# Products of the identity with itself, put on TensorE's queue at four changes of stage

## The chip, the core and the metric

The kernel runs on one core of a Trainium2 chip, as one launch. The metric is the device time of that launch in microseconds (us), the median of several runs. In the profile the engines are called PE (TensorE, its matrix products), PEld (TensorE's weight loads), DVE (VectorE), ACT (ScalarE), POOL (GpSimd) and SP (SyncE, which here only issues DMAs).

## What is computed

Two blocks of a network on 256 tokens of width 1024, in float32. The first block is windowed attention and pooling. The second has two layers, and its context of another 256 tokens runs beside the latent tokens. Layer 0 mixes by retention and gated linear attention, layer 1 by attention inside a window. Both layers end in the same two steps, and here the change sits:

```python
def second_block(x, c, ctx, c_ctx, ...):
    for i in range(2):
        h  = x  * (1 + sc1)  + sh1
        hc = xc * (1 + csc1) + csh1
        y  = mixer(h, hc)                 # layer 0: retention and GLA, layer 1: window attention
        x  = layer_norm(alpha * x + g1 * y, ...)
        x  = layer_norm(alpha * x + g2 * (square(relu((x * (1 + sc2) + sh2) @ w1)) @ w2), ...)
        # layer 0 does the same two lines for xc
    return x
```

## The kernel before, in words

**Products.** Every large weight is loaded as float32 (`raw`), cast on ACT into a high part `whi` and subtracted on DVE into a low part `wlo` (lines 135 and 136). Activations are split in the same way. A product of two such pairs is three matrix products, `mm3` (lines 159 to 161). `gemm_b` makes tokens x columns for one tile T of 128 tokens, `col_part` makes columns x tokens. Products that accumulate have a bank of PSUM each: `bank(tag)` gives one of 3 banks `mm`, 2 banks `S`, 2 banks `T` and 1 bank `O`.

**Order.** The program is written engine-free, and a scheduler sets each engine's order from the order of writing and from its own estimate of when operands are ready. TensorE then takes its products in that order. `tc.issue_after(x)` is the one instrument that pins: what is issued under it stands behind `x` on its engine. `queued[...]` keeps the last instruction of a kind for that use.

**The step between two stages.** A residual tile is normalised on DVE (`ln_stats` line 360, `ln_norm` line 374, with the power -0.5 on POOL in between). `modulate` (line 333 on) turns it for the next products: eight transposes on TensorE in two lots of four, each lot into a bank `T` (line 195); ACT scales and shifts them out of the bank into `hf` (line 342); DVE makes the high part (line 345) and the low part (line 346) of `h`. Token tiles 0 and 1 are the context, 2 and 3 the latent tokens.

**The four places.** I call them A to D.

- A, start of the MLP of layer 0. `proj_out` ends with the transposes of tiles 0, 1 and 2 (`mod0`); then the first products of `up(0)` run into four banks `os_` (two `mm`, two `S`), context half first; tile 3 is transposed in between.
- B, start of layer 1. The MLP of layer 0 ends with tiles 2 and 3 normalised and modulated, then tiles 0 and 1 are normalised (`normed(0)`, `normed(1)`) and `after(0)` modulates tile 0 (`y` in the profile's names). Layer 1 begins with K for the latent tokens into the banks `kb_` (`mm<-hCh,whi`), V for tiles 2 and 3 (`mm<-whi,hCh`), then K and V for the context and Q for the first heads (`rot_q(0)`, `rot_q(1)`). Tile 1 is modulated inside that stage. `put_q` moves Q by DMA (`Q<-qr`).
- C, the first `window` of attention: scores of Q with K into two banks `S` (line 1289), softmax on DVE and ACT (lines 1296 to 1308), transposes, products with V (line 1316).
- D, start of the MLP of layer 1. `proj_out` gives tiles 2 and 3 (`r`), `mod2` modulates tile 2 inside it and tile 3 behind it. `up(0)` makes tokens x 512 columns by `gemm_b` for tile 2, then for tile 3 (`mm<-whi,hDh`), takes relu and square on ACT (`f`, lines 1067 and 1068), transposes them (`T<-ident,f`) and splits them into `fx`. `down(0)` multiplies `fx` by the second weight.

Of the kernel before, what the change touches and what calls it, by code (L numbers as in the profile page):

```python
# [19 lines left out]
P = 128  # L20
D = 1024
S = 256
# [73 lines left out]
def body(tc, a, cst, out):  # L96
    nc = tc.nc
    with ExitStack() as ctx:
# [7 lines left out]
        def bank(tag):  # L106
            return psum.tile([P, 512], F32, tag=tag, name=tag, bufs={"mm": 3, "S": 2, "T": 2, "O": 1}[tag])
# [13 lines left out]
        queued = {}  # L121
# [35 lines left out]
        def mm3(o, lhs, rhs, first, last):  # L157
            (lh, ll), (rh, rl) = lhs, rhs
            nc.tensor.matmul(o, lh, rh, start=first, stop=False)  # L159
            nc.tensor.matmul(o, lh, rl, start=False, stop=False)  # L160
            queued["mm"] = nc.tensor.matmul(o, ll, rh, start=False, stop=last).ins  # L161

        def col_part(o, ws, j, xs_):

# [11 lines left out]
        def gemm_b(ws, xh, xl, t):  # L176

            n = ws[0][0].shape[-1]
            o = bank("mm")[:, :n]
            for k, w in enumerate(ws):  # L180
                mm3(o, (xh[:, k, t * P:(t + 1) * P], xl[:, k, t * P:(t + 1) * P]), w, k == 0, k == len(ws) - 1)
            return o
# [8 lines left out]
        ident = const.tile([P, P], F32, tag="ident", name="ident")  # L191
        neghalf = const.tile([P, 8], F32, tag="neghalf", name="neghalf")

        def transpose(o, i, n=P):
            return nc.tensor.transpose(o, i, ident[:n, :n])  # L195

        def rsqrt(v, n):

# [131 lines left out]
            nc.vector.tensor_add(B, B, sh[:, :, vec])  # L330
            return A, B

        def modulate(z, cols, dst, t0):

            A, B = cols
            for c in range(0, KC, 4):
                pt = bank("T")
                hf = tmp([P, 4, P], "hf")
                for i in range(4):
                    transpose(pt[:, i * P:(i + 1) * P], z[:, (c + i) * P:(c + i + 1) * P])  # L340
                for i in range(4):
                    queued["hf"] = nc.scalar.activation(hf[:, i, :], pt[:, i * P:(i + 1) * P], AF.Identity, scale=A[:, c + i:c + i + 1],  # L342
                                                        bias=B[:, c + i:c + i + 1]).ins
                hi, lo = (t[:, c:c + 4, t0:t0 + P] for t in dst)
                nc.vector.tensor_copy(hi, hf)
                queued["mod"] = nc.vector.tensor_sub(lo, hf, hi.bitcast(F32)).ins  # L346
# [183 lines left out]
        for g in range(3):  # L530
            oh = tmp([33, 384], "oh")
            nc.gpsimd.dma_start(oh, cst["oh"][:, g, :])
            pt = bank("S")
# [18 lines left out]
        for g in range(3):  # L552
# [4 lines left out]
            for i in range(2):  # L557
                o = gemm_a(w_in, 1536 * g + 256 * i, xk) if g else first[i].rearrange("p (j n) -> p j n", j=2)
# [112 lines left out]
        for i in range(2):  # L671
# [3 lines left out]
            for j in range(2):  # L675
                g = 2 * i + j
# [374 lines left out]
        def mlp(layer, Ts, xks, y, pool, mid, late, norm, after):  # L1051


            n = len(Ts) * P
            w1, w2 = a["mlp_w1_2"][layer], a["mlp_w2_2"][layer]
            def up(g):

                if g == 3:
                    rate[0] = 3
                fx = (main, pool)[g % 2].tile([P, 8, n], F32R, tag=("qkb", "fx")[g % 2], name="fx")  # L1060
                fh, fl = fx[:, 0:4], fx[:, 4:8]
                if layer and g < 1:
                    ws = w_b(w1, 512 * g)
                    for i in range(2):
                        o = gemm_b(ws, *h2, i)
                        f = pool.tile([P, 512], F32, tag="f", name="f", bufs=2)
                        nc.scalar.activation(f, o, AF.Relu)
                        nc.scalar.activation(f, f, AF.Square)
                        pt = bank("T")
                        for c in range(4):  # L1070
                            transpose(pt[:, c * P:c * P + P], f[:, c * P:c * P + P])
                        tv = pt.rearrange("p (c n) -> p c n", c=4)
                        split(fh[:, :, i * P:i * P + P], fl[:, :, i * P:i * P + P], tv)
                os_ = [bank("mm" if i < 2 else "S")[:, :n] for i in range(4)] if not layer and g == 0 else None
                if not layer and g == 0:
                    ws = [w_a(w1, 256 * i) for i in range(2)]
                    for part, xk_ in xks[0]:
                        for i in range(2):
                            for j in range(2):
                                col_part(os_[2 * i + j][:, part], ws[i], j, xk_)  # L1080
                            mid()
                for i in range(0 if layer and g < 1 else 2):
                    if g:
                        ws = w_a(w1, 512 * g + 256 * i)
                    for j in range(2):
                        if g:
                            o = bank("mm")[:, :n]
                            col_part(o, ws, j, xks[1])
                        else:
                            o = os_[2 * i + j]  # L1090
                        f = pool.tile([P, n], F32, tag="f", name="f", bufs=2)
                        nc.scalar.activation(f, o, AF.Relu)  # L1092
                        nc.scalar.activation(f, f, AF.Square)
                        split(fh[:, 2 * i + j, :], fl[:, 2 * i + j, :], f)
                with tc.issue_after(queued["split"]):
                    late(g)
                if g == 0:
                    rate[0] = 2
                return fh, fl

            def down(g, fh, fl, behind):

                for half in range(2):
                    ws = w_b(w2[512 * g:512 * g + 512, :], 512 * half, 4)
                    hs = slice(512 * half, 512 * half + 512)
                    for i, T in enumerate(Ts):
                        with tc.issue_after(behind) if behind else nullcontext():
                            o = gemm_b(ws, fh, fl, i)
                        if g == 0:
                            nc.vector.tensor_copy(y[:, T, hs], o)  # L1110
                        else:
                            nc.vector.tensor_add(y[:, T, hs], y[:, T, hs], o)  # L1112

            for g in range(6):
                down(g, *up(g), None)
            f6 = up(6)
            if layer:
                fh, fl = up(7)
                down(6, *f6, queued["mm"])
            else:  # L1120
                down(6, *f6, None)
                fh, fl = up(7)
            g = 7
            for T in Ts:
                nc.vector.tensor_mul(y[:, T, :], y[:, T, :], (gc, gx)[T // 2])
                nc.vector.scalar_tensor_tensor(y[:, T, :], resid(T), alpha, y[:, T, :], op0=ALU.mult, op1=ALU.add)
            ws = [w_b(w2[512 * g:512 * g + 512, :], 512 * half, 4) for half in range(2)]
            sts, ends = {}, []

            def products(T, half):  # L1130

                with tc.issue_after(ends[-2]) if len(ends) > 1 else nullcontext():
                    o = gemm_b(ws[half], fh, fl, Ts.index(T))
                ends.append(queued["mm"])
                gate_add(y, o, T, slice(512 * half, 512 * half + 512))

            def normed(T):
                norm(y[:, T, :], ln_stats(y[:, T, :], 1, ln_stats(y[:, T, :], 0)))

            for T in Ts[-2:]:  # L1140
                for half in range(2):
                    products(T, half)
                normed(T)
            if len(Ts) > 2:
                after(2)
                for T in Ts[:2]:
                    products(T, 0)
                after(3)
                for T in Ts[:2]:
                    products(T, 1)  # L1150
                with tc.issue_after(queued["mod"]):
                    normed(0)
                    normed(1)
                after(0)
# [8 lines left out]
        cc = mod_cols("c0b", 2, 6, m0["sc2"], m0["b"][:, 8:16], 1)  # L1163
        cx = mod_cols("x0b", 2, 6, m0["sc2"], m0["b"][:, 8:16], 0)
        h1 = new_h("hB")
        mod0 = lambda T: modulate(r0[:, T, :], (cc, cx)[T // 2], h1, P * T)
        proj_out(r0, a["ev_w_out_2"][0], yH, yL, range(4), mod0)
        lg.close()

# [89 lines left out]
        kT = gc.rearrange("p (j n) -> p j n", j=2)  # L1259
        vN = p4.tile([P, 4, 256], F32, tag="vN", name="vN")  # L1260
        wk, wv = w_a(wq, 1024), w_a(wq, 1280)
        kb_ = [bank("mm"), bank("mm")]
        KK = slot("A0", "KK", [P, 2, 2, 2, 512], F32R)
        for half, xk_ in ((1, hx), (0, hc)):
            hs = slice(S * half, S * half + S)
# [17 lines left out]
        def window(kv, c, qt):  # L1283

            qs = slice(P * qt, P * qt + P)
            sp = [bank("S"), bank("S")]
            for e in range(2):
                for part in range(2):
                    queued["qk"] = nc.tensor.matmul(sp[e], Q2[:, kv % 2, e, c % 2, qs], KK[:, part, kv // 2, kv % 2, :], start=part == 0, stop=part == 1).ins  # L1289
# [109 lines left out]
```

## Time and profile before

| | us |
|---|---|
| median of three runs | 1318.32 |
| the three runs | 1313.48, 1318.32, 1324.63 |
| the profiled execution | 1323.18 |
| its span, first to last instruction | 1321.4 |
| PE busy in that span | 1272.4 |
| DVE busy | 869.6 |
| ACT busy | 590.6 |
| mean granted TensorE clock, 1 is full speed | 0.981 |

The profile is of one execution. The span is what the rows below are measured in; 1.8 us of that execution lie around it. The granted clock is 1 at 2.4 GHz and 0.5 at 1.2 GHz; a value between means that the stretch had both. A matrix product's row gives its own time, which overlaps with the next one's: back to back, the distance from start to start is what a product costs.

### The profile page before, as it was taken

To read this page: it belongs to the slowest core of one execution; us is meant where nothing else is said; L and a number is where in the kernel's file an instruction comes from. 1 tells how busy PE (TensorE), PEld (TensorE's weight loads), DVE (VectorE), ACT (ScalarE), POOL (GpSimd) and SP (SyncE) were. 2 spreads that over 40 slices of the span, in tenths; PEclk is the share of its full clock that TensorE was granted. 3 is DMA by queue.
4 is the path that set the end of the run, shared out by engine and by line. 5 is a ranking of instruction groups with operands and counts; after the bars stand their busy time and mean duration, and the time that the engine had idled before them with its cause. 6 is when DMAs were issued, how large, how long until landed. Compare 5 with 4: busy or idle time off the path is not lost. (4 is left out here: it accounts for less than half of the span.)

```text
span 1321.4 us, 19813 instructions
## 1 busy us (share of the span) xinstructions
PE 1272.4 (96%) x7777; PEld 1045.9 (79%) x7777; DVE 869.6 (66%) x1344; ACT 590.6 (45%) x957; POOL 85.6 (6%) x148
## 2 busy tenths in 40 slices
PE   6999999999999999998999999999998899999996
PEld 5889845998887777778777777777888776788894
DVE  3568844696643357675868876677597677566567
ACT  4434534445431453326334333323445796655660
POOL 2010031000102100001010000000010000000000
PEclk9999969999999999998999999999999999999998
DMA  9789877675441412325656556664345214465651
GB/s 326 263 299 346 271 221 228 206 235 160 148 127 31 127 40 65 128 67 168 201 174 204 163 190 207 207 207 160 96 137 163 71 55 155 150 190 180 187 178 46
DMA packets 140964, 223.80 MB, mean 169 GB/s; under 512 B 8748, under 2 KB 88796, under 8 KB 140870
## 3 DMA queue, kind: packets, MB, share of 16 engines
q1 hardware_dynamic: 134832, 207.64, 49.2%
q0 software_dynamic: 5296, 14.33, 3.6%
q8 instruction: 61, 1.00, 0.3%
q10 hardware_dynamic: 742, 0.55, 0.1%
q14 instruction: 33, 0.27, 0.1%
HBM read 218.23 MB, written 1.12 MB: 166 GB/s over the span
## 5 line engine op out<-in xcount | busy, mean ns | idle before, releaser
L135 ACT CAST whi<-raw 128x1024 fp32r<-128x1024 f32 x261 | 272.9, 1051 | 372.8 <-PE mm L161 203.5
L136 DVE TENSOR_TENSOR wlo<-raw,whi 128x1024 fp32r<-128x1024 f32 x261 | 317.4, 1222 | 162.4 <-ACT whi L135 160.0
L159 PE MATMUL mm<-whi,fx 128*128 128x512 f32 x384 | 153.2, 399 | 2.6 <-DVE y L1112 1.2
L160 PE MATMUL mm<-wlo,fx 128*128 128x512 f32 x384 | 151.4, 395 | 0.0
L161 PE MATMUL mm<-whi,fx 128*128 128x512 f32 x384 | 147.4, 396 | 0.0
L288 DVE SCALAR_TENSOR_TENSOR mva<-mvraw,cst_m,mva 128x1024 f32<-128x1024 f32 x98 | 123.3, 1280 | 0.2
L160 PE MATMUL mm<-A1a,whi 128*128 128x256 f32 x352 | 99.8, 284 | 0.0
L159 PE MATMUL mm<-A1a,whi 128*128 128x256 f32 x352 | 99.8, 283 | 0.0
L161 PE MATMUL mm<-A1a,wlo 128*128 128x256 f32 x352 | 99.6, 283 | 0.0
L160 PE MATMUL mm<-hBl,whi 128*128 128x512 f32 (+1 forms) x256 | 98.4, 384 | 0.1
L159 PEld LDWEIGHTS mm<-whi,fx 128*128 128x128 f32 x384 | 72.2, 188 | 25.1 <-DVE y L1112 6.0
L161 PEld LDWEIGHTS mm<-whi,fx 128*128 128x128 f32 x384 | 72.2, 188 | 17.6 <-DVE fx L111 0.4
L160 PEld LDWEIGHTS mm<-wlo,fx 128*128 128x128 f32 x384 | 72.3, 188 | 16.0
L160 PEld LDWEIGHTS mm<-A1a,whi 128*128 128x128 f32 x352 | 66.2, 188 | 2.4 <-issue 2.3
L111 DVE TENSOR_TENSOR fx<-f,fx 128x512 fp32r<-128x512 f32 (+1 forms) x60 | 34.0, 566 | 51.5 <-ACT fx L110 51.3
L159 PEld LDWEIGHTS mm<-A1a,whi 128*128 128x128 f32 x352 | 66.4, 189 | 1.2 <-issue 1.0
L161 PEld LDWEIGHTS mm<-A1a,wlo 128*128 128x128 f32 x352 | 66.3, 188 | 0.8 <-issue 0.8
L1112 DVE TENSOR_TENSOR y<-y,mm 128x512 f32<-128x512 f32 x72 | 47.1, 683 | 28.2 <-PE mm L161 28.1
L160 PE MATMUL mm<-hDl,whi 128*128 128x256 f32 x224 | 63.1, 282 | 0.0
L1092 ACT ACTIVATE f<-mm 128x512 f32<-128x512 f32 (+1 forms) x58 | 28.4, 490 | 73.0 <-PE mm L161 73.0
L160 PEld LDWEIGHTS mm<-hBl,whi 128*128 128x128 f32 x256 | 48.8, 191 | 10.7 <-DVE hBl L346 0.4
L159 PE MATMUL mm<-whi,hA 128*128 128x512 f32 x128 | 51.2, 401 | 0.0
(519 smaller groups left out, 2846.2 us busy)
## 6 DMA issues: line engine op xcount, KB each, us to landing
raw<-in_mlp_w_dram SPq DMA_DIRECT2D x128, 512.0 KB, 4.1
mvraw<-in_w_mod_dram SPq DMA_DIRECT2D x96, 512.0 KB, 4.7
raw<-in_w_in_dram SPq DMA_DIRECT2D x64, 512.0 KB, 5.4
raw<-in_ev_w_in_dram SPq DMA_DIRECT2D x25, 512.0 KB, 3.9
raw<-in_od_w_qkv_dram SPq DMA_DIRECT2D x12, 512.0 KB, 3.5
mvraw<-in_w_ada_dram SPq DMA_DIRECT2D x10, 512.0 KB, 6.4
raw<-in_w_out_dram SPq DMA_DIRECT2D x8, 512.0 KB, 4.7
raw<-in_ev_w_out_dram SPq DMA_DIRECT2D x8, 512.0 KB, 4.4
```

The lines of the kernel that those rows point to most:

```text
L111: queued["split"] = nc.vector.tensor_sub(lo, src, hi.bitcast(F32)).ins
L135: nc.scalar.copy(hi, raw)
L136: queued["lo"] = nc.vector.tensor_sub(lo, raw, hi.bitcast(F32)).ins
L159: nc.tensor.matmul(o, lh, rh, start=first, stop=False)
L160: nc.tensor.matmul(o, lh, rl, start=False, stop=False)
L161: queued["mm"] = nc.tensor.matmul(o, ll, rh, start=False, stop=last).ins
L288: nc.vector.scalar_tensor_tensor(acc, raw, stat[:, k, m:m + 1], acc, op0=ALU.mult, op1=ALU.add)
L1092: nc.scalar.activation(f, o, AF.Relu)
L1112: nc.vector.tensor_add(y[:, T, hs], y[:, T, hs], o)
```

## The change

`awake(n, o, behind)` issues n products of the 128 x 128 float32 identity with itself into a bank `o` whose contents are overwritten afterwards; they stand behind the instruction `behind` on TensorE. They are issued at six points of the four places: A gets 6 before the first and 3 before the second lot of four transposes of tile 2 (banks `S`), and 2 before the first product of `up(0)`; B gets 5 before the first product into `kb_`; C gets 8 before the first scores; D gets 4 before the first product of `up(0)`. `behind` is `queued["last"]`, which `mm3` sets at its last product, and `modulate` at each transpose. At A the transposes of tile 2 are pinned behind the identity products too. The products accumulate into the same bank, so they stay behind the identity products that write it.

```diff
 def mm3(...):
-            queued["mm"] = nc.tensor.matmul(o, ll, rh, start=False, stop=last).ins
+            queued["mm"] = queued["last"] = nc.tensor.matmul(o, ll, rh, start=False, stop=last).ins
 def gemm_b(...):
-            o = bank("mm")[:, :n]
+            o = mm_bank()[:, :n]
...
+        ahead = []
+
+        def awake(n, o, behind):
+
+            with tc.issue_after(behind):
+                for _ in range(n):
+                    w = nc.tensor.matmul(o[:, :P], ident, ident, start=True, stop=True).ins
+            return w
+
+        def mm_bank():
+            o = bank("mm")
+            if ahead:
+                awake(ahead.pop(0), o, queued["last"])
+            return o
...
-        def modulate(z, cols, dst, t0):
+        def modulate(z, cols, dst, t0, keep=(0, 0)):
...
+                if keep[c // 4]:
+                    with tc.issue_after(queued["T"]):
+                        queued["awake"] = awake(keep[c // 4], bank("S"), queued["last"])
                 for i in range(4):
-                    transpose(pt[:, i * P:(i + 1) * P], z[:, (c + i) * P:(c + i + 1) * P])
+                    with tc.issue_after(queued["awake"]) if keep[c // 4] else nullcontext():
+                        queued["T"] = queued["last"] = transpose(pt[:, i * P:(i + 1) * P], z[:, (c + i) * P:(c + i + 1) * P]).ins
 def up(g):
                 if layer and g < 1:
+                    ahead.append(4)
...
-                os_ = [bank("mm" if i < 2 else "S")[:, :n] for i in range(4)] if not layer and g == 0 else None
+                if not layer and g == 0:
+                    ahead.append(2)
+                    os_ = [(mm_bank() if i < 2 else bank("S"))[:, :n] for i in range(4)]
...
-        mod0 = lambda T: modulate(r0[:, T, :], (cc, cx)[T // 2], h1, P * T)
+        mod0 = lambda T: modulate(r0[:, T, :], (cc, cx)[T // 2], h1, P * T, (6, 3) if T == 2 else (0, 0))
...
-        kb_ = [bank("mm"), bank("mm")]
+        ahead.append(5)
+        kb_ = [mm_bank(), mm_bank()]
...
             sp = [bank("S"), bank("S")]
+            if (kv, c, qt) == (0, 0, 0):
+                awake(8, sp[0], queued["last"])
```

What the scheduler makes of it shows in the order of the engines. At place B, on PE, before: the last products of the MLP of layer 0 (`fx`), the second lot of four transposes of tile 3 (`y`), and then at once products of layer 1 (`hCh` and `hCl` are its operand, tiles 2 and 3 of it).

```order
L160 MATMUL mm<-wlo,fx 128x512
L161 MATMUL mm<-whi,fx 128x512
L195 MATMUL T<-ident,y_5688 128x128 x4
L159 MATMUL mm<-hCh_8358,whi 128x256 x2
L159 MATMUL mm<-whi,hCh_8358 128x256
L160 MATMUL mm<-wlo,hCh_8358 128x256
L161 MATMUL mm<-whi,hCl 128x256
```

The same place with the change:

```order
L160 MATMUL mm<-wlo,fx 128x512
L161 MATMUL mm<-whi,fx 128x512
L195 MATMUL T<-ident,y_5699 128x128 x12
L203 MATMUL mm<-ident 128x128 x5
L159 MATMUL mm<-hCh_8371,whi 128x256
L160 MATMUL mm<-hCl,whi 128x256
L161 MATMUL mm<-hCh_8371,wlo 128x256
```

The eight transposes of tile 0, which stood 96 products later, have moved ahead of all products of layer 1 (four and eight make the twelve). The order of DVE up to the normalisation of tile 0 is the same in both.

At place D, on PE, before: the last products of `up(0)` for tile 2 (`hDh0b`, `hDl`), the eight transposes of tile 3 (`r`), the four of tile 2's `f`, and the products for tile 3.

```order
L160 MATMUL mm<-wlo,hDh0b 128x512
L161 MATMUL mm<-whi,hDl 128x512
L195 MATMUL T<-ident,r_9841 128x128 x8
L195 MATMUL T<-ident,f 128x128 x4
L159 MATMUL mm<-whi,hDh_9847 128x512
L160 MATMUL mm<-wlo,hDh_9847 128x512
```

With the change, what stands behind the last products of `proj_out` (`aHL`):

```order
L160 MATMUL mm<-wlo,aHL 128x512
L161 MATMUL mm<-whi,aHL 128x512 x2
L195 MATMUL T<-ident,r_9867 128x128 x8
L203 MATMUL mm<-ident 128x128 x4
L159 MATMUL mm<-whi,hDh_9873 128x512
L160 MATMUL mm<-wlo,hDh_9873 128x512
L161 MATMUL mm<-whi,hDl 128x512
```

The transposes of tile 3 have moved ahead of the 24 products of tile 2, and the four transposes of tile 2's `f` behind all 48 products. Of ACT at the same place the changed order has this; it had the first copy `fx<-T` ahead of the three casts:

```order
L1378 COPY xs<-r_9867 128x1024 x2
L1087 ACTIVATE f<-mm 128x512
L1088 ACTIVATE f<-f 128x512
L135 CAST whi<-raw 128x1024 x3
L1087 ACTIVATE f<-mm 128x512
L135 CAST whi<-raw 128x1024
L110 CAST fx<-T 128x4x128
L1088 ACTIVATE f<-f 128x512
```

The copy of tile 2's `fx` now stands behind tile 3's relu and a cast of a weight. At A and C the identity products are set in, and the order around them is otherwise nearly as it was. Inside stage B the products of Q for the first heads stand 96 products before the first scores (81 before), and in the attention stage some transposes, products with V and DMAs of Q have changed places by a few rows.

## Rows read from the trace of the kernel before

**Rows 1.** The page: PE's busy time in the span, and the granted clock in 40 slices.

```profile
PE 1272.4 (96%) x7777; PEld 1045.9 (79%) x7777; DVE 869.6 (66%) x1344; ACT 590.6 (45%) x957; POOL 85.6 (6%) x148
...
PEclk9999969999999999998999999999999999999998
```

**Rows 2.** Stretches at A, B, C, D: length, busy us (count) by engine, granted clock, DMA.

```profile
core 0: us, PE busy (x) PEld busy (x) DVE busy (x) ACT busy (x) POOL busy (x), PEclk, DMA share, GB/s
599.00:607.00 8.00, 6.42 (x32) 5.49 (x31) 7.25 (x14) 3.85 (x12) 1.27 (x1) 0.57 1.01 371
975.00:997.00 22.00, 19.41 (x153) 18.16 (x152) 19.89 (x42) 13.25 (x30) 1.44 (x2) 1.00 0.31 103
1015.00:1024.00 9.00, 6.93 (x42) 6.58 (x42) 6.50 (x14) 3.91 (x9) 0.00 (x0) 0.81 0.66 192
1114.00:1140.00 26.00, 21.71 (x84) 16.07 (x83) 18.18 (x26) 16.12 (x28) 1.09 (x2) 0.87 0.62 216
```

**Rows 3.** Timeline of PE at A: start, duration, operation, [idle before <- releaser].

```profile
598.72 0.66 PE L195 MATMUL T<-ident,r 128*128 128x128 f32 x4 [2.22 <-ACT hf L342]
600.11 1.12 PE L195 MATMUL T<-ident,r 128*128 128x128 f32 x4 [0.74 <-ACT hf L342]
601.95 0.79 PE L159 MATMUL mm<-hBh,whi 128*128 128x256 f32 x2 [0.72 <-DVE hBh L345]
...
603.67 0.42 PE L161 MATMUL mm<-hBh,wlo 128*128 128x256 f32 x1
...
606.41 0.28 PE L159 MATMUL mm<-hBh,whi 128*128 128x256 f32 x1
606.53 0.28 PE L160 MATMUL mm<-hBl,whi 128*128 128x256 f32 x1
```

**Rows 4.** Timeline of PE: eight full float32 products, 128 x 128, and what follows.

```profile
409.46 1.95 PE L835 MATMUL T<-yg,vx 128*128 128x128 f32 x16
411.16 0.47 PE L159 MATMUL mm<-whi,hA 128*128 128x512 f32 x1
```

**Rows 5.** Timeline of PE at B.

```profile
975.44 0.60 PE L195 MATMUL T<-ident,y 128*128 128x128 f32 x4
...
988.32 1.04 PE L195 MATMUL T<-ident,y 128*128 128x128 f32 x8
```

**Rows 6.** Timeline of DVE at B: the first of the two normalisations, tile 0.

```profile
985.48 0.81 DVE L374 TENSOR_SCALAR y<-y,mvst,rs_y 128x1024 f32<-128x1024 f32 x1 [0.54 <-POOL rs_y L200]
```

**Rows 7.** Timeline of PE at C and in the first windows behind it.

```profile
1017.99 1.16 PE L1289 MATMUL S<-KK,Q 128*128 128x512 f32 x4 [2.06 <-DMA Q<-qr]
...
1032.46 1.41 PE L1289 MATMUL S<-KK,Q 128*128 128x512 f32 x4 [1.30 <-DVE m L1296]
1035.89 1.71 PE L195 MATMUL T<-ident,pr 128*128 128x128 f32 x8 [2.03 <-DVE den L1302]
```

**Rows 8.** Timeline of ACT: Q of the first heads leaves its bank.

```profile
1007.19 0.58 ACT L1229 ACTIVATE A1t<-mm 128x512 f32<-128x512 f32 x1
```

**Rows 9.** Timeline of PE at D.

```profile
1114.34 0.64 PE L161 MATMUL mm<-whi,aHL 128*128 128x512 f32 x2
...
1124.59 1.09 PE L195 MATMUL T<-ident,r 128*128 128x128 f32 x8
1127.34 0.66 PE L195 MATMUL T<-ident,f 128*128 128x128 f32 x4 [1.66 <-ACT hf L342]
```

**Rows 10.** Timeline of DVE at D: the normalisation of tile 3.

```profile
1123.72 0.81 DVE L374 TENSOR_SCALAR r<-r,mvst,rs_y 128x1024 f32<-128x1024 f32 x1 [0.68 <-POOL rs_y L200]
```

**Rows 11.** Timeline of ACT at D: relu, a weight's cast, the copy of `fx`.

```profile
1135.51 0.60 ACT L1067 ACTIVATE f<-mm 128x512 f32<-128x512 f32 x1 [0.35 <-PE mm L161]
1136.01 1.04 ACT L135 CAST whi<-raw 128x1024 fp32r<-128x1024 f32 x1
...
1138.73 0.58 ACT L110 CAST fx<-T 128x512 fp32r<-128x512 f32 x1 [1.15 <-PE T L195]
```

## The prediction

> **What bounds the kernel now.** First I read the busy times and the granted clock on the page [rows 1]: PE is busy 96% of the span, so the kernel ends when PE has done its products, and only two things can be won: PE's waits, and the slices in which the clock is below full speed. The clock is the second reading, by stretches [rows 2]. From the mean clock of a stretch follows how long it stood at 1.2 instead of 2.4 GHz: (1 - clock) x length / 0.5. That is 6.9 us at A, none at B, 3.4 us at C and 6.8 us at D (two times 3.4 there). Each of these follows a time in which PE mostly waited. The same rows give the waits, length less busy: 2.6 us at B, 2.1 us at C, 4.3 us at D. Third I read PE's timeline there, to see what the waits are for, and DVE's, to see when that is ready.
>
> **What the half clock costs at most.** At A products of 256 columns follow each other 13 times between 603.67 and 606.41, which is 0.21 us each; right behind it they take 0.12 us [rows 3]. So a stretch at half clock that is full of products gives back 1 - 0.12/0.21 = 0.43 of its length.
>
> The Trainium skill has a shorter rule: on the page "TensorE: Matmul & The Clock Gate", section "Terms", the penalty is about the throttled time times the share of clock that is missing, here half. That would be 3.4 us at A, where the rows give 1.2 us, because for most of that stretch PE stood waiting and a slower clock cost nothing. I take the rows; the rule's result is a rival below.
>
> **The change, part by part.**
>
> *An identity product.* The trace has none, but it has full 128 x 128 float32 products: each is two records, and eight of them (16 records) take from 409.46 to 411.16, 1.70 us, so 0.21 us each at full clock [rows 4]. At half clock I take twice that, 0.43 us. The lower bound is zero, where a wait hides it.
>
> *A, 6 + 3 + 2.* They take 1.3, 0.6 and 0.4 us. The waits in which they stand are 2.22, 0.74 and 0.72 us, for ACT and DVE [rows 3], so they delay nothing; without that cover, all eleven cost 2.3 us. If the clock stays up, the four transposes at 600.11 no longer take 1.12 us, but the first product still waits for DVE until about 602, and its next operands until 603.3. What is won is the run from 603.67 to 606.41: 13 x 0.09 = **-1.2 us**.
>
> *B, 5, and C, 8.* Here the change does more than add. The identity products must stand behind the last instruction noted, and that is the last transpose of tile 0, written before layer 1 begins. So those eight transposes stand ahead of all products of layer 1 now (the order shows it). Before, PE was done with tile 3 at 975.44 + 0.60 = 976.0 [rows 5], and the products of K and V ran until the transposes of tile 0 at 988.32. These need tile 0 normalised, which DVE finishes at 985.48 + 0.81 = 986.3 [rows 6]. DVE's order up to there is unchanged, and nothing in it waits for the products that are now held up. So PE stands still for 986.3 - 976.0 = **+10.3 us**, and behind the waiting transpose are queued the 5 identity products, 288 products of K, V and Q, and the scores, for which DVE and ACT wait. What goes is the 2.6 us of waits that stood in 975 to 997 [rows 2], since tile 0 is now early, and I take it that the wait of 2.06 us for Q goes too [rows 7]: Q left its bank at 1007.19 [rows 8], 10.8 us before the scores started, and 96 products x 0.12 = 11.5 us now stand between. Net +5.6 us.
>
> With that no wait is left for the 5 and the 8 to stand in: 13 x 0.21 = +2.8 us. After a stall of ten us I expect PE to begin at half clock, as after the much shorter waits before. Eight transposes then cost 0.9 us more (four take 1.12 instead of 0.66 [rows 3]), five identity products 1.1 us more, some first products 0.3: +2.3 us. The 3.4 us at half clock behind the first scores, full of products, go: 3.4 x 0.43 = -1.5 us. B and C together: 5.6 + 2.8 + 2.3 - 1.5 = **+9.2 us**.
>
> *D, 4.* The same happens: the transposes of tile 3 now stand ahead of tile 2's products. PE is done with `proj_out` at 1114.34 + 0.64 = 1115.0 [rows 9]; tile 3 is normalised at 1123.72 + 0.81 = 1124.5 [rows 10]. Before, 24 products lay in that time, and the transposes followed them without a wait (1124.59). Now PE stands still for 9.5 us. All waits of 1114 to 1140, 4.3 us, go in exchange [rows 2], among them the 1.66 us before `f` [rows 9]: +5.3 us. The 4 identity products: +0.9 us. Start at half clock: 0.9 for the transposes, 0.9 for the identity products, 0.3 for the first others, +2.0 us. A new wait: behind the last product of tile 3 PE transposes tile 2's `f`, then needs its copy, and ACT now does relu, a cast and only then that copy, 0.60 + 1.04 + 0.58 = 2.2 us [rows 11], 0.3 of it beside the transposes: +1.9 us. The two stretches at half clock go: 6.8 x 0.43 = -2.9 us. D: 5.3 + 0.9 + 2.0 + 1.9 - 2.9 = **+7.2 us**.
>
> *The rest.* A few rows change places in the attention stage, and DMAs of Q stand one or two weight loads further ahead on SP's queue; I price that at zero, with 2 us to either side. POOL's order is the same.
>
> *Sum.* -1.2 + 9.2 + 7.2 = +15.2 us. Against the profiled execution, 1323.18 us (1321.4 of span and 1.8 around it), this gives 1338.4; the profiled execution is 4.9 us above the median of the three runs, which lie 11 us apart, so for the median it is 1318.3 + 15.2 = **1333.5 us**, 1.2% slower. A measurement of this kernel can tell about 1% from no change, 13.2 us; the forecast lies just beyond it.
>
> **Rivals.**
>
> *It does only what it says* (1313). The normalisations might come as early as the products did, so that the moved transposes hold nothing up. Then the identity products lie in waits and the half clock goes: -1.2 - 1.5 - 2.9 = -5.6, 1312.7 us. For it: the waits at A are just longer than the products put into them. Against it: the end of tile 0 on DVE at 986.3 and of tile 3 at 1124.5, each behind DVE work that needs nothing from PE. This is the case that is not slower; it decides if PE's wait before the moved transposes is under some 3 us in each place.
>
> *The attention stage takes part of it back* (1328.7). In the first windows PE waits 1.30 and 2.03 us for DVE's softmax [rows 7], and one more stretch at half clock follows. If DVE has worked off its casts while PE stood still at B, these go: 3.3 + 3.4 x 0.43 = 4.8 us, 1333.5 - 4.8. For it: two casts now stand ahead of the first softmax. Against it: most of these casts wait for buffers that PE's products set free, so they are late as PE is.
>
> *The clock stays low for longer after the stalls* (1337). At A it was low for 6.9 us, more than 4 us of it after the first product [rows 2, 3]. If it is so at B and D, some 4 us more of products run at half clock in each place: 2 x 4 x 0.43 = 3.4, 1336.9 us. Against it: three of the stretches lasted 3.4 us.
>
> *The half clock costs more than the products show* (1330.6). Half of each low stretch at A, C and D, 3.4 + 1.7 + 3.4 = 8.5 us, would then come back instead of 5.6 us: 1333.5 - 2.9. Against it: PE waited for operands in the stretch at A [rows 3]. The page of the Trainium skill named above gives that rule.
>
> **How the numbers follow.** Chances: forecast 0.40, only what it says 0.07, attention takes back 0.25, clock low for longer 0.20, the higher price of the clock 0.08. The runs before lie 11 us apart, so each case has some 5 us to either side. Slower by over 1% (beyond 1331.5) takes 0.26 of the forecast's 0.40, 0.19 of the longer low clock, 0.02 of the attention's and 0.03 of the last: 0.50. Faster by over 1% (below 1305.1) has 0.02 from the edge of the first rival. Within 1% is left with 0.48. The range goes from 1317, which leaves most of the first rival out and holds the lower edge of the attention's, to 1344, which is the case of a longer low clock with the 2 us of the rest and an upper bound of the identity products (17 at half clock, 17 x 0.21 = 3.6, less the 2 counted).
>
> **What would show it.** In the changed profile, one wait of PE of about 10 us for DVE's normalisation before transposes of `y` near 976 to 986, one of about 9.5 us before transposes of `r`, each with a clock near 0.5 behind it; no wait for `Q<-qr`; no low clock at A; waits of ACT `hf` and DVE `hCh` after 990 gone; a wait of about 2 us for ACT's copy `fx`. I am wrong if these two waits are under 5 us, if the clock does not fall behind them, or if the time from B to the first scores grows by less than 5 us.

## The result, and the profile after

The changed kernel takes 1332.53 us, the median of four runs (1331.67 to 1333.61), against 1318.26 us before, again four runs (1313.48 to 1324.63). The ratio is 1.0114, with a 95% interval of 1.0083 to 1.0144: 14.3 us slower. The profiled execution took 1333.61 us, its span is 1331.8 us. Over the whole span PE's busy time did not grow, it is 1271.5 us against 1272.4 [rows 1], and the mean clock rose from 0.981 to 0.983. That compares two executions whose first blocks differ by themselves: from 172 to 196 us the granted clock is 0.89 here and was 0.57 in the profile of before, in work that the change doesn't touch. From stage A to D of the table below the span grew by 14.2 us; PE stands still for 30.1 us there against 19.1, so 11.0 us of the loss are time in which PE waits, and 3.2 are work.

The page of the changed kernel, PE's busy time and its clock in 40 slices:

```profile
PE 1271.5 (95%) x7833; PEld 1050.9 (79%) x7833; DVE 871.3 (65%) x1344; ACT 591.4 (44%) x957; POOL 85.4 (6%) x148
...
PEclk9999989999999999999999999999989898999998
```

The stretches that [rows 2] show of before, and behind them the two waits and what follows each of them:

```profile
core 0: us, PE busy (x) PEld busy (x) DVE busy (x) ACT busy (x) POOL busy (x), PEclk, DMA share, GB/s
599.00:607.00 8.00, 7.41 (x64) 7.40 (x64) 3.57 (x7) 1.32 (x5) 1.27 (x1) 1.00 0.74 282
975.00:997.00 22.00, 15.56 (x115) 15.60 (x116) 12.67 (x31) 6.21 (x18) 1.44 (x2) 0.77 0.14 44
1114.00:1140.00 26.00, 15.59 (x84) 12.94 (x83) 14.01 (x23) 12.25 (x25) 1.61 (x3) 0.80 0.55 196
971.04:981.43 10.39, 0.00 (x1) 0.03 (x1) 9.78 (x20) 3.93 (x7) 1.44 (x2) 0.73 0.55 173
981.43:985.16 3.73, 3.73 (x19) 3.73 (x19) 1.73 (x3) 2.55 (x8) 0.00 (x0) 0.50 0.00 0
985.00:990.00 5.00, 5.00 (x40) 5.00 (x39) 2.26 (x7) 0.89 (x3) 0.00 (x0) 0.90 0.00 0
1118.80:1129.20 10.40, 0.00 (x0) 0.03 (x1) 8.90 (x15) 3.07 (x6) 1.08 (x2) 0.68 0.94 339
1129.20:1132.51 3.31, 3.31 (x17) 3.31 (x17) 0.61 (x2) 2.18 (x7) 0.00 (x0) 0.50 0.17 58
```

At A the clock is now full. At B PE is idle for 10.39 us and at D for 10.40 us, DVE is busy for nearly all of it at B, and in each case the clock falls inside the wait and is at its lower level, 1.2 GHz, while the work behind it starts. The timeline of PE names the waits. First A, which answers to [rows 3]:

```profile
592.65 1.50 PE L203 MATMUL S<-ident 128*128 128x128 f32 x12
595.04 0.66 PE L195 MATMUL T<-ident,r 128*128 128x128 f32 x4 [0.88 <-ACT hf L361]
595.53 0.83 PE L203 MATMUL S<-ident 128*128 128x128 f32 x6
596.43 0.66 PE L195 MATMUL T<-ident,r 128*128 128x128 f32 x4
596.92 0.61 PE L203 MATMUL mm<-ident 128*128 128x128 f32 x4
598.26 0.51 PE L159 MATMUL mm<-hBh,whi 128*128 128x256 f32 x2 [0.73 <-DVE hBh L364]
```

The identity products (`ident` alone, two records each) stand in the waits and delay nothing: the two lots of four transposes start 1.39 us apart, as before (600.11 - 598.72 [rows 3]), and both lots of four transposes take 0.66 us, where the second took 1.12 [rows 3]. Now B with C and D, still PE; these answer to [rows 5, 7, 9]:

```profile
970.44 0.60 PE L195 MATMUL T<-ident,y 128*128 128x128 f32 x4
981.43 1.94 PE L195 MATMUL T<-ident,y 128*128 128x128 f32 x8 [10.39 <-DVE y L393]
983.16 2.34 PE L203 MATMUL mm<-ident 128*128 128x128 f32 x10
985.16 0.56 PE L159 MATMUL mm<-hCh,whi 128*128 128x256 f32 x1
...
1020.70 1.95 PE L203 MATMUL S<-ident 128*128 128x128 f32 x16
1022.40 1.17 PE L1314 MATMUL S<-KK,Q 128*128 128x512 f32 x4
...
1034.19 1.41 PE L1314 MATMUL S<-KK,Q 128*128 128x512 f32 x4 [0.34 <-DVE m L1321]
1037.63 1.94 PE L195 MATMUL T<-ident,pr 128*128 128x128 f32 x8 [2.03 <-DVE den L1327]
...
1118.16 0.64 PE L161 MATMUL mm<-whi,aHL 128*128 128x512 f32 x2
1129.20 1.94 PE L195 MATMUL T<-ident,r 128*128 128x128 f32 x8 [10.41 <-DVE r L393]
1130.94 1.92 PE L203 MATMUL mm<-ident 128*128 128x128 f32 x8
1132.51 0.62 PE L159 MATMUL mm<-whi,hDh 128*128 128x512 f32 x1
...
1143.89 0.60 PE L195 MATMUL T<-ident,f 128*128 128x128 f32 x4
1146.16 0.50 PE L159 MATMUL mm<-whi,fx 128*128 128x512 f32 x1 [1.67 <-ACT fx L110]
```

Line 393 is the normalisation (374 before), 1314 the scores (1289), 203 the identity products. The moved transposes wait for DVE's normalisation; the eight take 1.73 us at B (981.43 to 983.16) where eight took 0.79 before (988.32 [rows 5] to the next product at 989.11); and the identity products behind them delay work that is ready. The wait for `Q<-qr` [rows 7] is gone: the scores follow the identity products at once.

Stage by stage, from the starts and ends of PE's rows (us; A runs from the start of the last row of `proj_out` of layer 0 to the end of the last product of that layer's MLP; B from there to the first scores, so it holds C's eight products; C from there to the start of the last row of `proj_out` of layer 1; D from there to the start of the 21st row of products with `fx`):

| kernel (name of the run) | A | B | C | D |
|---|---|---|---|---|
| before | 380.4 | 42.4 | 96.4 | 27.0 |
| after | 379.1 | 51.8 | 95.8 | 33.7 |
| order_alone | 380.9 | 49.7 | 96.5 | 32.3 |
| no_move | 379.0 | 43.3 | 93.6 | 25.2 |
| b_back | 379.0 | 42.3 | 93.8 | 33.3 |
| fill | 379.0 | 49.6 | 96.7 | 31.7 |
| d_back | 379.1 | 51.1 | 95.1 | 25.4 |
| lean | 379.0 | 43.8 | 93.8 | 24.9 |
| lean_c24 | 379.0 | 46.5 | 93.5 | 24.9 |
| lean_more | 379.0 | 42.6 | 94.4 | 24.9 |
| before_again | 380.5 | 44.1 | 94.7 | 25.5 |
| after_again | 379.1 | 51.7 | 95.7 | 33.2 |

Between before and after these are -1.3, +9.4, -0.6 and +6.7 us, together 14.2.

### The profile page after: what moved, and what is told of

It reads as the page before. It is cut to its first block, busy times and chain, and to the rows that moved or that the text cites. A ratio compares the mean times of both kernels' runs of the same rounds, so it can differ in the third digit from the quotient of the medians.

```text
span 1331.8 us, 19924 instructions
## 1 busy us (share of the span) xinstructions
PE 1271.5 (95%) x7833; PEld 1050.9 (79%) x7833; DVE 871.3 (65%) x1344; ACT 591.4 (44%) x957; POOL 85.4 (6%) x148
## 3 DMA queue, kind: packets, MB, share of 16 engines
HBM read 218.23 MB, written 1.12 MB: 165 GB/s over the span
## 4 chain that ended last, share of the span: by engine, by line
PE 66%; DVE 5%; issue 1%; DMA 1%; ACT 1%; POOL 0%; DVEq 0%; ACTq 0%
PE mm L159 19%; PE mm L160 18%; PE mm L161 18%; PE T L195 2%; PE O L1341 1%; DVE wlo L136 1%; DMA raw<-in_mlp_w_dram 1%; PE S L1314 1%; PE T L854 1%; DVE y L1134 0%; PE S L842 0%; PE O L309 0%; DVE st L379 0%; PE S L160 0%; ACT whi L135 0%
```

## Experiments

Three theories. *Order*: the two waits of PE before the moved transposes cost the time. *Products*: the 28 identity products and what they disturb cost it. *Clock*: the waits are paid back later, and the half clock behind them is what stays. The kernels of the first four runs were timed beside 18 runs of before with a median of 1316.78 us, the next four beside 35 in all with a median of 1317.01 us. Each difference below is to the runs beside it. The four runs of before in the result lie a little higher: against the 35, the changed kernel's 1332.53 us are 15.5 us more instead of 14.3.

### order_alone: the moved transposes with almost no identity products

```diff
-ahead.append(4)              # D
+ahead.append(1)
...
-ahead.append(2)              # A
...
-mod0 = lambda T: modulate(..., (6, 3) if T == 2 else (0, 0))   # A
+mod0 = lambda T: modulate(..., (0, 0))
...
-ahead.append(5)              # B
+ahead.append(1)
...
-if (kv, c, qt) == (0, 0, 0):       # C
-    awake(8, sp[0], queued["last"])
```

> One identity product in place of five at B and one in place of four at D, so that both pins stay; none at A and none at C. Order theory (the two waits before the moved transposes cost the time): the gain at A is not had (+1.2 us against the changed kernel), four products at half clock go at B (-1.7), eight at C (-1.7), three at D (-1.3). That is 3.5 us under the changed kernel, about 1329 us, 11 us above before, with both waits of about 10 us in the trace. Product theory (the identity products and what they disturb cost it): with 26 of 28 gone, within 3 us of before, about 1320 us. Clock theory (what counts is the half clock behind the waits, the waits themselves are paid back by waits that vanish): about 1329 us as well, this run does not tell it from the first.

Measured: 1329.46 us, ratio 1.0100 (1.0075 to 1.0126), 12.7 us over before. PE's timeline at B and at D:

```profile
979.32 1.94 PE L195 MATMUL T<-ident,y 128*128 128x128 f32 x8 [10.39 <-DVE y L393]
...
1125.11 1.94 PE L195 MATMUL T<-ident,r 128*128 128x128 f32 x8 [9.70 <-DVE r L393]
```

With 2 of the 28 products nine tenths of the loss are there, and so are the waits. The product theory falls.

### no_move: all the products, no moved transposes

```diff
-queued["T"] = queued["last"] = transpose(...).ins
+queued["T"] = transpose(...).ins
+if keep[c // 4]:
+    queued["last"] = queued["T"]
```

> All 28 identity products, but transposes no longer set the instruction behind which they stand (only the pinned ones at A do), so at B and D they stand behind the last product of the stage before and move no transposes. Order theory: A -1.2, C -1.5 (the eight stand in the wait for Q), D -1.4 (four stand in a wait of 0.9 us and the first of the two low stretches goes), B up to +1.1 (five products without a wait to stand in): 3 us under before, about 1315 us, and no wait of 10 us. Product theory: the products are all there, so at least two thirds of the loss stays, over 1327 us. Clock theory: as the order theory, since the waits go and with them the half clock.

Measured: 1314.28 us, ratio 0.9976 (0.9952 to 0.9999), 2.5 us under before. PE at B and at D:

```profile
970.75 1.28 PE L203 MATMUL mm<-ident 128*128 128x128 f32 x10
971.87 0.60 PE L195 MATMUL T<-ident,y 128*128 128x128 f32 x4
...
1108.19 1.05 PE L203 MATMUL mm<-ident 128*128 128x128 f32 x8
1109.23 0.50 PE L159 MATMUL mm<-whi,hDh 128*128 128x512 f32 x1
```

The products are the same 28, the waits of 10 us are gone, and the loss has turned into a small gain. (Some products of layer 1 and rows of the attention stage have changed places against before as well; lean, below, has the order of before.) At D the four fill the wait of 0.88 us that stood before the first product of `hDh`: none is noted before it now. At B the five cost their 1.1 us (970.75 to 971.87), since nothing is waited for there: 43.3 against 42.4 us.

### b_back and d_back: one of the two pins left out

```diff
-ahead.append(5)              # b_back
```

> The five identity products at B are left out and with them the pin there; A, C and D as in the changed kernel. Order theory: A -1.2, C -1.5 (the wait for Q is back and the eight stand in it), D +7.2: 4.5 us above before, about 1323 us. Product theory: 23 of 28 products are left, some 12 us above before, about 1330 us. Clock theory: the restart at B goes, 2.3 us, and little else: about 1330 us.

```diff
-ahead.append(4)              # d_back
```

> The four identity products at D are left out and with them the pin there; A, B and C as in the changed kernel. Order theory: the stage of D was 6.7 us longer in the changed kernel than before and is as before now, so about 1326 us, 7.6 us above before, with the wait at B in the trace and none at D. Product theory: 24 of the 28 products are left, 12 us above before, about 1330 us.

Measured: b_back 1322.02 us, ratio 1.0046 (1.0029 to 1.0063), 5.2 us over before where the order theory said 4.5. d_back 1323.03 us, ratio 1.0045 (1.0013 to 1.0076), 6.0 us where it said 7.6. Each has the one wait and not the other:

```profile
1117.04 1.94 PE L195 MATMUL T<-ident,r 128*128 128x128 f32 x8 [9.70 <-DVE r L393]
```

(b_back, and no wait over 1.3 us at B), and

```profile
976.04 1.94 PE L195 MATMUL T<-ident,y 128*128 128x128 f32 x8 [10.40 <-DVE y L393]
```

(d_back). The two places hardly touch each other: in the table b_back has the B of before and about the D of after, d_back the reverse. By the medians 14.3 - 5.2 = 9.1 us of the loss hang on the pin at B and 14.3 - 6.0 = 8.3 on that at D; their sum is 3.1 us above 14.3, which would be what the other edits gain. That agrees with lean, below, which gains about as much with both pins gone, but the intervals of these two runs reach 2 and 4 us to either side, so it is no more than consistent.

### fill: the waits filled with identity products

```diff
-modulate(y0[:, T, :], ..., P * T)                       # after0
+modulate(y0[:, T, :], ..., P * T, (46, 0) if T == 0 else (0, 0))
...
-modulate(r1[:, T, :], cx, h2, P * (T - 2))              # mod2
+modulate(r1[:, T, :], cx, h2, P * (T - 2), (46, 0) if T == 3 else (0, 0))
```

> The order of the changed kernel, and 46 identity products more ahead of the moved transposes of tile 0 at B and of tile 3 at D, in the waits of about 10 us. Order theory: the transposes still wait for the normalisation until the same time; only the half clock behind it goes, 2.3 us at B and 2.0 us at D by the forecast: about 1328 us, with a granted clock of 1 behind both. Clock theory: nearly all of the loss goes, 1318 to 1322 us. Product theory: 92 more at 0.21 us are 19 us, about 1350 us.

Measured: 1329.56 us, ratio 1.0094 (1.0061 to 1.0127). The stretches of B and D, and PE's rows there:

```profile
975.00:997.00 22.00, 21.89 (x191) 21.73 (x190) 14.57 (x33) 8.34 (x22) 1.44 (x2) 1.00 0.16 49
1114.00:1140.00 26.00, 26.00 (x179) 23.42 (x176) 14.97 (x23) 14.22 (x26) 1.62 (x3) 1.00 0.51 181
```

```profile
972.08 10.44 PE L203 MATMUL S<-ident 128*128 128x128 f32 x92
982.63 1.06 PE L195 MATMUL T<-ident,y 128*128 128x128 f32 x8
...
1127.43 1.06 PE L195 MATMUL T<-ident,r 128*128 128x128 f32 x8
1128.33 1.06 PE L203 MATMUL mm<-ident 128*128 128x128 f32 x8
1129.14 0.47 PE L159 MATMUL mm<-whi,hDh 128*128 128x512 f32 x1
```

PE is busy throughout and the clock stays at 2.4 GHz, and the transposes of tile 0 still start 10.8 us after the end of the MLP's last product (971.8 to 982.63; 970.61 to 981.43 in the changed kernel). It is DVE that they wait for and not the 46 products ahead of them: in both kernels they start 0.95 us behind the start of DVE's row of the normalisation (981.67 here, 980.48 in the changed kernel), and so do those of tile 3 at D (1126.47 and 1127.43 here, 1128.25 and 1129.20 there). What goes is the restart at half clock alone. At B it was worth 51.79 - 49.64 = 2.15 us. At D the transposes and identity products take 1.71 us (1127.43 to 1129.14) where they took 3.31 (1129.20 to 1132.51), 1.6 us less; the stage as a whole is 2.0 us shorter, but that figure is not clean, since the scheduler put 7 of the 46 among the last products of `proj_out`, and a stretch at half clock came later in the stage. The clock theory falls: the waits of about 10 us are paid whatever the clock does.

### lean: the products where they move nothing

This is no_move without the five at B. Its order of PE from B to D is that of before with eight and four products set in, but for two products of layer 1 at B that stand earlier.

> As the run without moved transposes, and B's five products left out too, so that the order is that of before with products set in at A, C and D. From the stages of the traces of the first four runs: A -1.3, C -2.5, D -1.8: 5 to 6 us under before, about 1311 us (order theory: where the products move nothing they gain what the half clock cost). Product theory: 23 products, no gain or a loss, 1317 us or more.

Measured: 1313.32 us over 12 runs, ratio 0.9971 (0.9946 to 0.9996), 3.7 us under before. Like no_move it lies under both kernels, by little. Its A, C and D are about the forecast ones against the first profile of before; at B its execution had a stretch at half clock of 3.4 us that this profile hadn't, 43.8 us against 42.4. Against the second profile of before (before_again in the table) C and D are only 0.9 and 0.6 us shorter, while A's gain, 1.4 and 1.5 us, is there against both.

### lean_c24: what a product costs that has no wait to stand in

```diff
-awake(8, sp[0], queued["last"])
+awake(24, sp[0], queued["last"])
```

> As lean, with 24 instead of 8 identity products at C. The wait there holds some nine of them. Order theory: an identity product past the wait costs its 0.21 us, 15 x 0.21 = 3.2 us above lean, and nothing more. Product theory: they disturb what follows, more than 5 us above lean. If the wait for Q is not what they stand in (they would be hidden anyway): within 1 us of lean.

Measured: 1315.82 us, ratio 0.9998 (0.9972 to 1.0024), 2.5 us above lean. PE before the first scores, in lean and in this one:

```profile
1010.66 1.95 PE L203 MATMUL S<-ident 128*128 128x128 f32 x16
1012.80 1.46 PE L1315 MATMUL S<-KK,Q 128*128 128x512 f32 x4 [0.19 <-DMA Q<-qr]
```

```profile
1015.09 5.52 PE L203 MATMUL S<-ident 128*128 128x128 f32 x48
1020.37 1.17 PE L1315 MATMUL S<-KK,Q 128*128 128x512 f32 x4
```

Eight and the rest of the wait take 2.14 us (1010.66 to 1012.80), 24 take 5.28 us: 3.14 us more, and the prediction's 0.21 us for a product gives (24 - 8) x 0.21 - 0.19 = 3.2. Here a product in a wait was free, and behind the end of the wait it cost its 0.21 or 0.22 us.

### lean_more: two more places

```diff
+if (kv, c, qt) == (0, 1, 1):            # first windows
+    awake(8, bank("mm"), queued["qk"])
...
+ahead.append(7)                          # and queued["last"] set in gla_out
 proj_out(r0, ...)
```

> As lean, with eight more in the first windows, in the wait of 2.0 us for the softmax behind which the second low stretch of the attention stage begins, and seven ahead of the output projection of layer 0, where a wait of 1.7 us for its operand has a low stretch of 3.4 us behind it. If the products keep the clock up there as at A, C and D: 1.4 us less at each, about 3 us under lean, 1308 us. If the softmax bounds those windows and not the products: the clock stays up and the time stays that of lean, 1311 us.

Measured: 1313.95 us over 12 runs, ratio 0.9979 (0.9956 to 1.0003): nothing more than lean. The clock stays at 1 in both places, from 225 us to the end of PE's work, and the stage C is 94.4 us against 93.8. Ahead of the projection of layer 0 the products did what they were to: from its first to its last product PE takes 48.73 us, 50.30 in lean. But the two profiles of before take 48.72 and 48.73 there, without any such product: the low stretch was no fixed part of the kernel. In the attention stage PE now waits where lean does not, for DVE:

```profile
1058.09 0.74 PE L1316 MATMUL S<-KK,Q 128*128 128x512 f32 x2 [0.64 <-DVE m L1325]
...
1095.32 1.09 PE L1345 MATMUL O<-PT,vN 128*64 128x128 f32 x16 [1.00 <-DVE aHL L111]
```

In all its waits behind the eight products that are over 0.3 us sum to 2.5 us, where lean's behind that place sum to 0.6. So the time kept at full clock in the first windows is at least partly waited off later in the stage. That the new order of its rows has a part in this isn't excluded.

### before_again and after_again: each kernel once more

Both are unchanged kernels, so there is no edit.

> The kernel before, unchanged, profiled a second time, to see which differences of the traces belong to the execution and not to a kernel. If the stretches at half clock belong to the kernel: the same seven as in the first profile, and the stages from the last product of the projection of layer 0 on within 0.3 us of it (380.4, 42.4, 96.4 and 27.0 us). If the clock behind a wait of 1 to 2 us falls in some executions and not in others: some of the low stretches missing or new ones, and stages that differ by 1.4 us or a multiple of it; the scatter of the runs, 1311 to 1331 us, then comes from there, above all from the stretch at 172 to 194 us, which no change touches.

> The changed kernel, unchanged, profiled a second time. Order theory: the two waits of 10.4 us again, since they depend on the order and on DVE, with the clock low behind each; stages of 379.1, 51.8, 95.8 and 33.7 us to 1.5 us. If the waits belong to the execution: they differ by more than 1 us.

Measured: 1314.80 and 1332.39 us. The changed kernel repeats itself, with waits of 10.39 and 9.70 us and stages within 0.5 us. The kernel before does not. Stretches of its first profile and then of its second, by the time of its own span: early in the kernel, in the first block; the waits at B; and, of the second profile, the first scores:

```profile
172.00:196.00 24.00, 24.00 (x85) 10.14 (x81) 6.70 (x23) 4.32 (x11) 4.04 (x9) 0.57 0.62 180
985.00:997.00 12.00, 9.84 (x80) 9.16 (x79) 9.96 (x22) 7.91 (x21) 1.32 (x2) 1.00 0.00 1
```

```profile
172.00:196.00 24.00, 23.91 (x127) 11.51 (x127) 12.18 (x41) 9.35 (x23) 5.61 (x10) 0.93 0.87 264
985.00:997.00 12.00, 10.57 (x73) 10.13 (x74) 7.02 (x11) 7.44 (x16) 0.00 (x0) 0.86 0.31 84
1009.00:1018.00 9.00, 6.76 (x54) 6.42 (x53) 6.04 (x14) 4.41 (x9) 0.00 (x0) 1.00 0.65 185
```

By (1 - clock) x length / 0.5 the first stretch was at half clock for 20.6 us in one execution and 3.4 us in the other. At B none and 3.4 us. At C 3.4 us [rows 2] and none, though the wait for `Q<-qr` there was 2.23 us now and 2.06 us then. So part of the low stretches belongs to the execution.

## Why the prediction was right

The forecast was 1333.5 us, 15.2 over before, slower; measured are 1332.53 us and 14.3 over before (15.5 over the 35 runs). The mechanism is the one that was forecast. That the sum is out by less than 1 us is in part luck: the interval of the ratio leaves 11 to 19 us, and below two misses of about 1 us have opposite signs. Its steps:

- *The waits.* Forecast 10.3 us at B and 9.5 us at D, before the moved transposes, for DVE's normalisation; measured 10.39 us at B, and 10.41 and 9.70 us at D in the two executions. Most of the 0.7 us between the latter stands in DVE's timeline: in the longer one a weight's subtraction (at 1125.30), queued ahead of the last statistics of tile 3, waits 0.61 us for ACT's cast, and in the other it doesn't wait. order_alone, b_back and d_back tie the loss to these waits.
- *The restart at half clock.* Forecast 2.3 and 2.0 us (the parts named for the latter make 2.1); fill, which leaves the waits and takes the restart away, gives 2.15 us at B and 1.6 us at D for the transposes and identity products, for which the forecast had 1.8.
- *The identity products.* Forecast 0.21 us at full clock, 0.43 at half; eight take 1.70 us at C (1020.70 to 1022.40), five take 2.00 us at B at half clock (983.16 to 985.16), 0.40 each. At A they delay nothing, as forecast.
- *A.* Forecast -1.2, measured -1.3 us (-1.4 between the second executions).
- *B and C.* Forecast +9.2, measured +9.4 - 0.6 = +8.8 us (+7.6 + 1.0 = +8.6 between the second executions). Up to the first scores the parts gave 5.6 + 2.8 + 2.3 = 10.7, and 9.4 were measured. PE's idle time there grew from 4.65 us (2.59 and 2.06 [rows 2, 7]) to 10.39, which is 5.7, as forecast. So the work grew by 9.4 - 5.7 = 3.7 us where 2.8 + 2.3 = 5.1 were forecast, 1.4 too much. That is the term of waits removed: each of the small waits that went also had a start and an end that the rows count as busy. The first product of K, for one, fills 0.38 us (at 975.84) before a wait of 0.22, where a product of its size costs 0.12 us back to back. fill comes to the same: its stage B, without the stretch of 10.55 us that is filled (972.08 to 982.63) and without 13 x 0.21 us of products, is 49.64 - 10.55 - 2.73 = 36.36 us of work at full clock, against 42.39 - 4.65 = 37.74 before, 1.4 less. No run isolates the single waits. Against it, C's low stretch was to give back 1.5 us, and the attention stage got 0.6: the wait of 1.30 us in the first windows shrank to 0.34, but the stretch at half clock behind the next one (2.03 us, as before) grew from 3.4 to 6.7 us by the clocks of 0.86 and 0.76 below. The two misses are of opposite sign. Of before and then of after, the windows behind that wait:

```profile
1034.00:1046.00 12.00, 10.11 (x77) 8.10 (x78) 8.27 (x26) 10.14 (x27) 0.00 (x0) 0.86 0.10 22
```

```profile
1034.00:1048.00 14.00, 11.78 (x73) 9.18 (x73) 9.82 (x31) 10.79 (x28) 0.00 (x0) 0.76 0.20 56
```

- *D.* Forecast +7.2, measured +6.7 us (+7.7 between the second executions). The idle time of the stage went from 4.3 to 12.3 us; it is the wait of 10.41, the new one for `fx` of 1.67 us, forecast 1.9, and 0.18.
- *What could show it wrong.* Both waits are over 5 us, the clock is low behind both, and the time from B to the first scores grew by 9.4 us.
- *The range.* 1317 to 1344 is wider than what is named for its ends: 1336.9 + 2 + 1.6 = 1340.5 at the top, and at the bottom the attention's 1328.7 less 5, which is 1323.7. The measured time lies inside either.

Of the rivals, "only what it says" described the kernel no_move and not this one: its 1312.7 us are near the 1314.28 and 1313.32 us of no_move and lean. "Attention takes it back" saw the shorter wait, but not what followed it. "The clock stays low for longer" is out for the changed kernel: from the start of the transposes on it was low for 3.7 us and one more at B, (1 - 0.90) x 5 / 0.5, and for 3.3 us and 0.3 more at D, where it is 0.90 from 1132.51 to 1134.00. It isn't out in general. In order_alone the clock stayed at its lower level for 4.0 us of layer 1's products behind the wait at B, 1.7 us by the price of 0.43:

```profile
981.34:985.32 3.98, 3.98 (x20) 3.98 (x20) 2.24 (x4) 2.06 (x6) 0.00 (x0) 0.50 0.00 0
```

So how much of the ready work meets the low clock varies as well. "The half clock costs more" would have A give back 3.4 us, where it gave 1.3. The Trainium skill's rule on the page "TensorE: Matmul & The Clock Gate", section "Terms", half of the throttled time here, is too much in this kernel: of the 10.1 us at half clock at B, (1 - 0.77) x 22 / 0.5, PE stood still in 5.6, (1 - 0.73) x 10.39 / 0.5, and fill gave back 2.15 us and not 5.1.

One thing of the prediction was sharper than it had a right to be: it took the stretches at half clock at C and D as fixed features of the kernel. The second profile of before has none at C's first scores and one at D.

## What to carry to other kernels

Pinning an instruction behind "the last one noted" moves that last one too: what is to go into a wait must be pinned behind work that is already ready there, or it drags something late to the head of an in-order queue. Look in the new order for what now stands ahead of the first ready work, and read from the trace when its operand comes: here that gave both waits, 10.3 and 9.5 us, before any run. Filler products can give back no more than what the half clock costs in work that was ready. Here a stretch of 3.4 us full of products cost 1.6 us (50.30 against 48.73 us in the projection of layer 0, with and without it), and at A, where one of 6.9 us had waits in it, keeping the clock up gave 1.3 us. From the end of the wait on a filler product cost 0.21 us.

## What was not expected

- The clock behind waits of 1 to 2 us falls in one execution of a kernel and not in the next: behind 1.20 us at B in the second profile of before and not in the first, behind the wait for Q (2.06 and 2.23 us) in the first and not in the second. In the waits of about 10 us that stood empty it fell every time: eight in five executions, two each in the two of the changed kernel and in order_alone, one each in b_back and d_back. The Trainium skill says on the page "TensorE: Matmul & The Clock Gate", section "What's actually happening", that the watch on PE's activity runs freely and is not started by the kernel; the two profiles of before agree with that, but no run here shows it by itself.
- Executions of one kernel differ most in work that the change doesn't touch. Up to the first product of the projection of layer 0 PE took 546.51 us in the first profile of before and 539.36 in the second, 7.2 us apart; the stretch from 172 to 196 us was at half clock for 17.2 us more, which at 0.43 is 7.4. The second had a stretch of its own near 20 us (a clock of 0.81 from 16 to 25 us, 1.00 in the first), 3.4 us long, so the two together account for at least 5.9. From the last product of that projection to PE's last product they are 1.2 us apart (712.61 and 711.37). For a change of 1% the stages say more than the whole, though B, C and D too differ by 1.5 to 1.7 us between the two executions.
